# High and low weight parts in one tile, and 57 groups of dummy products behind the work

## The chip, the cores and the metric

The kernel runs on one core of one Trainium2 chip. A core has five engines that run their own instruction queues beside each other: TensorE (PE in the profile, its weight loads are PEld), VectorE (DVE), ScalarE (ACT), GpSimd (POOL) and SyncE (SP, which here only issues DMAs). They share a memory of 128 partitions (SBUF); TensorE writes its products into a second memory, PSUM, in banks of 512 float32 columns. The metric is the device time of one execution in microseconds.

## The reference

Input is a residual stream `x` of 256 rows by 4096 columns in float32. One layer runs: a normalisation, a projection to four times 4096 columns, attention with 32 heads of 128, a gate, a projection back, the residual sum, and a last normalisation.

```python
h = x + attn_branch(rms_norm(x, norm_attn), w_in_attn, w_out_attn)   # DEPTH = 1
return rms_norm(h, final_norm)

def attn_branch(xn, w_in, w_out):
    proj = xn @ w_in                       # 256 x 4096 by 4096 x 16384
    q, k, v, g = jnp.split(proj, 4, axis=-1)
    o = stick_breaking_attention(to_heads(q), to_heads(k), to_heads(v))
    return (o * jax.nn.silu(g)) @ w_out    # 256 x 4096 by 4096 x 4096
```

Nearly all of the arithmetic lies in the two large products. The convolution layer of the source isn't reached with one layer.

## The kernel before

**Products in three.** Each float32 operand is split in a high part, rounded to TensorE's 32-bit type `F32R`, and a low part, which is the rest. A product of two float32 tiles is then three products: high by high, the moving operand's low part by the stationary operand's high part, and the reverse (`mm3`). The stationary operand is a 128x128 block of the input rows ("forms": `sh`, `sl`, later `oh`, `ol`), the moving operand 512 columns of weights (`wh`, `wl`). Most steps use seven instead of eight block products, by a Strassen-like scheme, with sums of weight tiles formed on VectorE and by adding DMAs.

**Units and parts.** There are 20 units of work (`units`): 16 over the columns of the first weight matrix and 4 over the second. A unit runs through 16 steps of the inner dimension, and each step through two to four "parts" of weights. `load` brings the raw tile (`raw`, a ring of 7) by DMA; `piece` (from `split`) has ScalarE write the high part `wh[n]` and VectorE the low part `wl[n]`; `product` multiplies. Parts of two inner blocks have tag `w` in a ring of 5 (`PAIRS`), parts of one have tag `s` in a ring of 2. In the kernel before, `wh` and `wl` are two tiles with tags of their own (`wh`, `wl` of 4 KB in a partition each, for the pairs).

**Order.** The class `Plan` writes out the order of the instructions of every engine: it runs a small simulation with assumed costs and due times, and emits an instruction when its engine is free. `keep_in_program_order` then pins each instruction behind the one before it on its engine. All of these have line 121 in the profile, so groups are told apart by tile names.

**The end.** In the last unit five parts, the last five of the pairs' ring (numbers 989 to 993 of all parts), are kept until the end (`KEPT`), and their products run block by block in the order `LAST_ORDER`, so that the four result blocks finish one after the other. `last_h`, `block_done`, `part_done` and `finish` add the residual, sum squares on ScalarE, form the factor of the last normalisation (a logarithm and an exponential on ScalarE, a Newton step on VectorE), scale the rows and store them, first for rows 128 to 255 (`t` = 1), then for rows 0 to 127.

Of the kernel before, what the change touches and what calls it, by code (L numbers as in the profile page):

```python
# [10 lines left out]
F32 = mybir.dt.float32  # L11
F32R = mybir.dt.float32r
BF16 = mybir.dt.bfloat16
AF = mybir.ActivationFunctionType
ALU = mybir.AluOpType
# [4 lines left out]
P = 128  # L20
# [5 lines left out]
CW = 256  # L26
HG = CW // P
NB = D // CW
W = 2 * CW
NJ = D // W  # L30
KT = 2
# [11 lines left out]
RAW_BUFS = 7  # L43
PAIRS = 5
# [193 lines left out]
def kernel(  # L238
# [10 lines left out]
    nc = Plan(tc)  # L249
# [3 lines left out]
    wp = ctx.enter_context(tc.tile_pool(name="weights", bufs=1))  # L253
    sp = ctx.enter_context(tc.tile_pool(name="stationary", bufs=1))
    dp = ctx.enter_context(tc.tile_pool(name="spill", bufs=1, space=DRAM))
    acc = ctx.enter_context(tc.tile_pool(name="acc", bufs=1, space=PSUM))
    att = ctx.enter_context(tc.tile_pool(name="att", bufs=1, space=PSUM))
    rooms = ExitStack()
    ap = rooms.enter_context(tc.tile_pool(name="attention", bufs=1))
# [40 lines left out]
    for g, (n, k) in enumerate(order):  # L300
        p = parts[n]
        b = p["u"], p["prods"][k][0]
# [51 lines left out]
    raw, wh, wl = {}, {}, {}  # L354
# [48 lines left out]
    def sums(q):  # L403

        a, b, c, d = quad_parts[q]
        one, two = raw[q, 0], raw[q, 1]
        for k in range(2):
            tile_left[q, k] += 1

        def add(to, at_, f, g, key, op=ALU.add):  # L410
            return dve(
                lambda: nc.vector.tensor_tensor(out=to[:, :, at_, :], in0=f, in1=g, op=op), W,
                key - SUMS_AHEAD * 1e3,
            )

        yield nc.until(("lows", a), ("T3", q))
        yield add(one, 0, one[:, :, 0, :], two[:, :, 0, :], first[c], ALU.subtract)
        yield nc.until(("lows", b))
        yield add(two, 1, one[:, :, 0, :], two[:, :, 1, :], first[c])
        nc.tell(("sums", c))  # L420
        yield add(one, 1, one[:, :, 0, :], one[:, :, 1, :], first[d])
        nc.tell(("sums", d))
        for k in range(2):
            tile_done(q, k)

    def piece(n, c, there):

        p = parts[n]
        yield nc.until(*there)
        full = raw[p["tile"]][:, :, p["place"], :][:, :, c, :].rearrange("p i c n -> p c i n")  # L430
        h, l = (t[n][:, c, :].rearrange("p c (i n) -> p c i n", i=HG) for t in (wh, wl))
        size = (c.stop - c.start) * W
        key = first[n] - (AHEAD * 1e3 if p["seven"] and p["i"] < 2 else 0)
        yield act(lambda: nc.scalar.copy(h, full), size, key - 2.0 * 1e3)
        if n == 0:
            yield nc.until(("sh", c.start))
        yield dve(lambda: minus(l, full, h), size, key)
        for k in range(c.start, c.stop):
            nc.tell(("low", n, k))
        low_done(n)  # L440

    def split(size, tag, bufs):
        for n, p in enumerate(parts):
            if p["size"] != size:
                continue
            q = p["quad"]
            yield nc.take(tag)
            t = p["tile"][1]
            yield nc.until(("raw", q, t))
            wh[n] = wp.tile([P, size, W], F32R, tag=tag + "h", name=f"wh{n}", bufs=bufs)  # L450
            wl[n] = wp.tile([P, size, W], F32R, tag=tag + "l", name=f"wl{n}", bufs=bufs)
            cuts = [slice(k, k + 1) for k in range(KT)] if n == 0 else [slice(0, size)]
            lows_left[n] = len(cuts)
            if p["seven"] and p["i"] == 0:
                nc.start(sums(q))
            for c in cuts:
                nc.start(piece(n, c, [("sums", n)] if p["seven"] and p["i"] > 1 else [("raw", q, t)]))
# [112 lines left out]
    for k in range(WARM):  # L570
# [10 lines left out]
        out=bound, in_=bound, compare_op=ALU.is_gt, fill=0.0, base=0,  # L581
# [6 lines left out]
        out=tri_f, in_=tri_f, compare_op=ALU.is_ge, fill=0.0, base=0, pattern=[[-1, P]], channel_multiplier=1,  # L588
# [465 lines left out]
    def last_h():  # L1054

        u, c = LAST, NJ - 2
        bank = ev.setdefault(u, {})
        key = place_of[u + 1, 0] - (KEPT * 4 + 8) * PRODUCT
        late = place_of[u + 1, 0]
        add = lambda to, f, g, k=late, n=W: dve(  # L1060
            lambda: nc.vector.tensor_tensor(out=to, in0=f, in1=g, op=ALU.add), n, k
        )
        for d in range(2):
            yield nc.until(("used", u, LAST_STEPS[d]))
            new_h(c + d)
        for d in range(2):
            yield nc.until(("used", u, LAST_STEPS[2 + d]))
            for t in range(NT):
                yield load_out(c + d, t)
        yield nc.until(("h", c - 1))  # L1070
        for d in range(2):
            yield nc.take("gh")
            yield load_gain(c + d)
        one, two = ([hs[c + d, t] for t in range(NT)] for d in range(2))
        yield nc.until(("full", u, 1))
        yield act(lambda: nc.scalar.copy(two[0], bank[1]), W, key)
        yield act(lambda: nc.scalar.copy(one[0], bank[1]), W, key)
        yield nc.until(("full", u, 6))
        yield add(two[0], bank[6], two[0], key)
        yield nc.until(("full", u, 7))  # L1080
        yield add(two[1], bank[7], two[0], key)
        yield act(lambda: nc.scalar.copy(one[1], two[1]), W, key)
        for t, b, d in ((1, 5, 1), (1, 4, 0), (0, 2, 0), (0, 3, 1)):
            nc.start(block_done(c + d, t, b, bank, add, key + 10 * (NT - 1 - t), late))
        yield nc.until("C22")
        yield add(two[0], bank[5], two[0], late - 1)
        nc.tell("C12")
# [109 lines left out]
    def products():  # L1197
        for g, (n, k) in enumerate(order):
# [18 lines left out]
            nc.here = g * PRODUCT  # L1217

    together(split(KT, "w", PAIRS), split(1, "s", SINGLES), products(), x_stats(), x_factor(), constants())

    def in_turn(works):
# [14 lines left out]
        nc.start(again(s))  # L1236
    nc.start(last_h())
    nc.run()


# [36 lines left out]
```

## Time and profile before

| | us |
|---|---|
| time, median of 2 runs | 1740.2 (1739.15 to 1741.24) |
| span of the profiled execution, first to last instruction | 1738.8 |
| TensorE busy in it | 1722.9, 7735 products |
| VectorE busy | 1643.5 |
| ScalarE busy | 1204.9 |
| GpSimd busy | 335.5 |

The span leaves out what lies before the first and behind the last instruction; the median lies 1.4 us above it. A product's "busy" time in the profile counts from its start to its modelled end, and products overlap, so the rate of TensorE is read from the distance of their starts.

### The profile page before, as it was taken

What the parts mean: (1) busy time and instruction counts of PE and PEld (TensorE: products, weight loads), DVE (VectorE), ACT (ScalarE), POOL (GpSimd) and SP (SyncE); (2) the same over time, 40 slices, a digit from 0 to 9 for tenths busy, and PEclk for the clock granted to TensorE, in tenths of its full rate; (3) what the DMA queues carried; (4) which work ended last, traced back from release to release, by engine and by line L of the source; (5) the groups of instructions that cost most, each with busy time, mean ns of one, the idle gap of its engine ahead of it and who ended that gap; (6) DMA issues with size and microseconds to landing.
All of it is one profiled execution on the core that took longest, in us unless ns stands there. A gap on an engine that the chain in (4) does not pass through costs nothing.

```text
span 1738.8 us, 24830 instructions
## 1 busy us (share of the span) xinstructions
PE 1722.9 (99%) x7735; PEld 1412.5 (81%) x7735; DVE 1643.5 (95%) x2106; ACT 1204.9 (69%) x1640; POOL 335.5 (19%) x407
## 2 busy tenths in 40 slices
PE   9999999999999999999999999999999999999997
PEld 6888888888888888888888888888888888878885
DVE  8889999999999999999999999999999987999997
ACT  7976767676767676767676767676767675666655
POOL 0022222222222221212222222222222112221220
PEclk9999999999999999999999999999999999999999
DMA  9967788878787878787878787878787878788895
GB/s 363 297 191 227 229 231 226 230 229 236 224 234 223 240 216 238 217 251 208 255 206 255 206 256 198 257 203 259 198 256 203 269 245 265 230 268 251 233 303 191
DMA packets 249380, 413.79 MB, mean 238 GB/s; under 512 B 28128, under 2 KB 73440, under 8 KB 249248
## 3 DMA queue, kind: packets, MB, share of 16 engines
q1 hardware_dynamic: 194544, 354.24, 60.6%
q0 software_dynamic: 54416, 57.70, 20.2%
q8 instruction: 60, 0.98, 0.2%
q14 instruction: 72, 0.59, 0.1%
q10 hardware_dynamic: 288, 0.28, 0.0%
HBM read 403.98 MB, written 8.13 MB: 237 GB/s over the span
## 4 chain that ended last, share of the span: by engine, by line
PE 78%; DVE 12%; issue 6%; ACT 2%; DMA 2%; SPq 0%; DVEq 0%; ACTq 0%
PE acc L121 74%; DVE wl L121 8%; DVE raw L121 3%; PE z L121 2%; PE o L121 1%; ACT wh L121 1%; DMA raw<-in_w_in_dram 1%; PE tr L121 1%; DVE gv_sb L121 1%; DVE h L121 0%; DMA raw<-in_w_out_dram 0%; DMA grow<-in_gain_out_dram 0%; DVE qk_sb L121 0%; SPq L121 0%; ACT sq L121 0%
## 5 line engine op out<-in xcount | busy, mean ns | idle before, releaser
L121 ACT CAST wh<-raw 128x1024 fp32r<-128x1024 f32 (+1 forms) x995 | 922.0, 971 | 406.1 <-issue 180.0
L121 DVE TENSOR_TENSOR wl<-raw,wh 128x1024 fp32r<-128x1024 f32 (+1 forms) x995 | 1068.8, 1123 | 58.4 <-ACT wh L121 56.6
L121 PE MATMUL acc<-wh,sh 128*128 128x512 f32 x1898 | 755.6, 398 | 0.0
L121 PE MATMUL acc<-wl,sh 128*128 128x512 f32 x1898 | 740.0, 390 | 0.8 <-DVE wl L121 0.8
L121 PE MATMUL acc<-wh,sl 128*128 128x512 f32 x1898 | 740.5, 390 | 0.0
L121 POOL DMA_DIRECT2D raw<-in_w_in_dram x300 | 262.9, 988 | 1078.9 <-DMA raw<-in_w_in_dram 427.4
L121 PEld LDWEIGHTS acc<-wh,sl 128*128 128x128 f32 x1898 | 356.3, 188 | 75.8 <-DVE sl L121 0.4
L121 PEld LDWEIGHTS acc<-wl,sh 128*128 128x128 f32 x1898 | 357.0, 188 | 73.8 <-DVE wl L121 2.8
L121 PEld LDWEIGHTS acc<-wh,sh 128*128 128x128 f32 x1898 | 356.8, 188 | 70.7 <-ACT wh L121 0.6
L121 DVE TENSOR_TENSOR raw<-raw,raw 128x512 f32<-128x512 f32 x354 | 243.4, 687 | 6.9 <-DMA raw<-in_w_out_dram 1.2
L121 PE MATMUL acc<-wl,oh 128*128 128x512 f32 x485 | 189.7, 391 | 2.0 <-DVE wl L121 1.8
L121 PE MATMUL acc<-wh,oh 128*128 128x512 f32 x485 | 190.0, 392 | 0.0
L121 PE MATMUL acc<-wh,ol 128*128 128x512 f32 x485 | 188.9, 389 | 0.0
L121 DVE TENSOR_TENSOR raw<-raw 128x512 f32<-128x512 f32 x177 | 121.0, 684 | 0.0
L121 PEld LDWEIGHTS acc<-wl,oh 128*128 128x128 f32 x485 | 91.1, 188 | 23.8 <-DVE wl L121 5.3
L121 PEld LDWEIGHTS acc<-wh,oh 128*128 128x128 f32 x485 | 91.0, 188 | 19.2 <-DVE gv_sb L121 0.5
L121 PEld LDWEIGHTS acc<-wh,ol 128*128 128x128 f32 x485 | 91.0, 188 | 18.8
L121 POOL DMA_DIRECT2D raw<-in_w_out_dram x54 | 47.1, 968 | 185.9 <-DVE wl L121 58.9
L121 ACT ACTIVATE f<-f 128x384 f32<-128x384 f32 x96 | 50.5, 526 | 3.0
L121 ACT COPY qkT<-tr 128x512 f32<-128x512 f32 x32 | 18.6, 581 | 24.1 <-PE tr L121 24.1
L121 ACT CAST oh<-p 128x512 fp32r<-128x512 f32 (+3 forms) x46 | 20.9, 467 | 18.8 <-DVE p L121 13.2
L121 DVE SCALAR_TENSOR_TENSOR gv_sb<-acc,rin_v,gv_sb 128x512 f32<-128x512 f32 x45 | 33.4, 741 | 0.0
(91 smaller groups left out, 750.3 us busy)
## 6 DMA issues: line engine op xcount, KB each, us to landing
raw<-in_w_in_dram SPq DMA_DIRECT2D x1024, 256.0 KB, 4.5
raw<-in_w_out_dram SPq DMA_DIRECT2D x256, 256.0 KB, 4.3
raw<-in_w_in_dram POOLq DMA_DIRECT2D x300, 128.0 KB, 4.7
p<-spill POOLq DMA_DIRECT2D x28, 256.0 KB, 4.2
raw<-in_w_out_dram POOLq DMA_DIRECT2D x54, 128.0 KB, 5.1
xr<-in_x_dram SPq DMA_DIRECT2D x16, 256.0 KB, 4.8
xres<-in_x_dram SPq DMA_DIRECT2D x16, 256.0 KB, 5.6
out_dram<-h SPq DMA_DIRECT2D x16, 256.0 KB, 2.8
```

The source lines that it names most:

```text
L121: return self.tc.keep_in_program_order(getattr(self.engine, name)(*args, **kw))
```

## The change

Two things change. In `split`, high and low part of one part of weights become the two halves of one tile with one tag (8 KB in a partition for the pairs, 4 KB for the others). Behind the plan's run, a new function `probes` is called: it clears a tile, fills from it a tile `m` of 2048 columns, a tile of stationary blocks `w`, and a third tile that is written six times by ScalarE and six times by VectorE in a spread order; then it issues 57 groups of 13 products into the bank with tag `b1`. Each group reads its moving operand out of `m` by another access pattern, a list of (step, count) pairs in elements, with an offset in some. All of `m` and `w` is zero, and no later instruction reads the results.

```diff
@@ split @@
-            wh[n] = wp.tile([P, size, W], F32R, tag=tag + "h", name=f"wh{n}", bufs=bufs)
-            wl[n] = wp.tile([P, size, W], F32R, tag=tag + "l", name=f"wl{n}", bufs=bufs)
+            both = wp.tile([P, 2, size, W], F32R, tag=tag, name=f"w{n}", bufs=bufs)
+            wh[n], wl[n] = both[:, 0], both[:, 1]
@@ tile_trunk_kernel, its end @@
     nc.run()
+    probes(tc.nc, wp, acc)
+
+LANES = [
+    [(1, 512)],
+    [(16, 128), (1, 4)],
+    [(16, 128), (1, 4), 4],
...
+    [(12, 128), (1, 4)],
+    [(8, 128), (1, 4)],
+    [(4, 2), (16, 64), (1, 4)],
...
+    [(1024, 2), (16, 64), (1, 4)],
...
+    [(16, 64), (8, 2), (1, 4)],
...
+    [(16, 42), (4, 3), (1, 4)],
...
+    [(0, 128), (1, 4)],
+    [(0, 64), (4, 2), (1, 4)],
...
+    [(0, 64), (1024, 2), (1, 4)],
+    [(0, 32), (16, 4), (1, 4)],
...
+    [(16, 64), (1, 6)],
+    [(4, 4), (16, 32), (1, 4)],
+    [(16, 96), (1, 4)],
+    [(16, 126), (1, 4)],
+    [(4, 2), (16, 63), (1, 4)],
+]
+AGAIN = 13
+
+def probes(nc, wp, acc):
+    zero = wp.tile([P, HG, KT, CW], F32, tag="raw", name="zero", bufs=RAW_BUFS)
+    nc.vector.memset(zero, 0.0)
+    zero = zero.rearrange("p i k n -> p (i k n)")
+    m = wp.tile([P, 4, W], F32R, tag="w", name="probe_m", bufs=PAIRS)
+    for k in range(2):
+        nc.scalar.copy(m[:, 2 * k : 2 * k + 2].rearrange("p k n -> p (k n)"), zero)
+    m = m.rearrange("p k n -> p (k n)")
+    w, r = (wp.tile([P, 4, W], F32R, tag="w", name=f"probe_{k}", bufs=PAIRS) for k in range(2))
+    w, r, r2 = (t.rearrange("p k n -> p (k n)") for t in (w, r[:, 0:2], r[:, 2:4]))
+    nc.scalar.copy(w[:, 0:1024], zero)
+    spread = lambda t: t.rearrange("p (h q e) -> p q h e", q=4, e=4)
+    for k in range(6):
+        nc.scalar.copy(spread(r), zero.rearrange("p (q h e) -> p q h e", q=4, e=4))
+    for k in range(6):
+        nc.vector.tensor_tensor(out=spread(r2), in0=zero.rearrange(...), in1=spread(r.bitcast(F32)), op=ALU.subtract)
+    out = acc.tile([P, W], F32, tag="b1", name="probe_out")
...
+    for dims in LANES:
+        a, shape = lanes(m, dims)
+        o = out[:, 0 : math.prod(shape)]
...
+        for k in range(AGAIN):
+            nc.tensor.matmul(o, w[:, 128 * (k % 2) : 128 * (k % 2) + 128], a, start=True, stop=True, skip_group_check=True)
```

Of the 57 groups, 47 have 512 columns, 8 have 504 and 2 have 384. In the first group the columns lie one behind the other; in all others the innermost runs are of 4 columns (6 in one group), and the patterns differ in the distance and the order of these runs.

More of the change, by code (lines that the diff above doesn't have):

```diff
@@ L1238 @@
     nc.run()
+    probes(tc.nc, wp, acc)
[3 more added lines that the diff above has]
+    [(16, 128), (1, 4), 4],
+    [(16, 128), (1, 4), 8],
+    [(16, 128), (1, 4), 12],
+    [(12, 128), (1, 4)],
+    [(8, 128), (1, 4)],
+    [(4, 2), (16, 64), (1, 4)],
+    [(4, 2), (16, 64), (1, 4), 8],
+    [(8, 2), (16, 64), (1, 4)],
+    [(12, 2), (16, 64), (1, 4)],
+    [(1024, 2), (16, 64), (1, 4)],
+    [(1028, 2), (16, 64), (1, 4)],
+    [(0, 2), (16, 64), (1, 4)],
+    [(16, 64), (1024, 2), (1, 4)],
+    [(16, 64), (1028, 2), (1, 4)],
+    [(16, 64), (8, 2), (1, 4)],
+    [(16, 64), (12, 2), (1, 4)],
+    [(16, 32), (512, 4), (1, 4)],
+    [(32, 64), (16, 2), (1, 4)],
+    [(32, 64), (20, 2), (1, 4)],
+    [(16, 42), (4, 3), (1, 4)],
+    [(4, 3), (16, 42), (1, 4)],
+    [(12, 42), (4, 3), (1, 4)],
+    [(0, 128), (1, 4)],
+    [(0, 64), (4, 2), (1, 4)],
+    [(0, 64), (8, 2), (1, 4)],
+    [(0, 64), (16, 2), (1, 4)],
+    [(0, 64), (32, 2), (1, 4)],
+    [(0, 64), (64, 2), (1, 4)],
+    [(0, 64), (128, 2), (1, 4)],
+    [(0, 64), (256, 2), (1, 4)],
+    [(0, 64), (512, 2), (1, 4)],
+    [(0, 64), (1024, 2), (1, 4)],
+    [(0, 32), (16, 4), (1, 4)],
+    [(0, 16), (16, 8), (1, 4)],
+    [(0, 8), (16, 16), (1, 4)],
+    [(0, 4), (16, 32), (1, 4)],
+    [(0, 32), (4, 4), (1, 4)],
+    [(0, 32), (8, 4), (1, 4)],
+    [(0, 32), (32, 4), (1, 4)],
+    [(0, 16), (32, 8), (1, 4)],
+    [(0, 16), (4, 8), (1, 4)],
+    [(0, 8), (4, 16), (1, 4)],
+    [(0, 16), (8, 8), (1, 4)],
+    [(16, 16), (4, 8), (1, 4)],
+    [(256, 8), (16, 16), (1, 4)],
+    [(512, 4), (16, 32), (1, 4)],
+    [(1536, 2), (8, 64), (1, 4)],
+    [(16, 42), (512, 3), (1, 4)],
+    [(16, 21), (336, 6), (1, 4)],
+    [(336, 6), (16, 21), (1, 4)],
+    [(16, 64), (1, 6)],
[4 more added lines that the diff above has]
+]
@@ new lines, with lanes @@
+AGAIN = 13
[14 more added lines that the diff above has]
+    for k in range(6):
+        nc.vector.tensor_tensor(
+            out=spread(r2), in0=zero.rearrange("p (q h e) -> p q h e", q=4, e=4), in1=spread(r.bitcast(F32)), op=ALU.subtract
+        )
+    out = acc.tile([P, W], F32, tag="b1", name="probe_out")
+    def lanes(t, dims):
+        at_ = 0
+        if not isinstance(dims[-1], tuple):
+            dims, at_ = dims[:-1], dims[-1]
+        a = t[:, at_ : at_ + 1]
+        return bass.AP(tensor=a.tensor, offset=a.offset, ap=[a.ap[0], *([s, n] for s, n in dims)]), [n for _, n in dims]
+    for dims in LANES:
+        a, shape = lanes(m, dims)
+        o = out[:, 0 : math.prod(shape)]
+        if len(shape) == 2:
+            o = o.rearrange("p (a b) -> p a b", b=shape[1])
+        if len(shape) == 3:
+            o = o.rearrange("p (a b c) -> p a b c", b=shape[1], c=shape[2])
+        for k in range(AGAIN):
+            nc.tensor.matmul(
+                o, w[:, 128 * (k % 2) : 128 * (k % 2) + 128], a, start=True, stop=True, skip_group_check=True
+            )
```

## The prediction

> **What bounds the kernel now.** First the page: busy shares and the chain that ended last.
>
> ```profile
> span 1738.8 us, 24830 instructions
> PE 1722.9 (99%) x7735; PEld 1412.5 (81%) x7735; DVE 1643.5 (95%) x2106; ACT 1204.9 (69%) x1640; POOL 335.5 (19%) x407
> ...
> PE 78%; DVE 12%; issue 6%; ACT 2%; DMA 2%; SPq 0%; DVEq 0%; ACTq 0%
> ...
> L121 PE MATMUL acc<-wh,sh 128*128 128x512 f32 x1898 | 755.6, 398 | 0.0
> L121 PE MATMUL acc<-wl,sh 128*128 128x512 f32 x1898 | 740.0, 390 | 0.8 <-DVE wl L121 0.8
> L121 PE MATMUL acc<-wh,sl 128*128 128x512 f32 x1898 | 740.5, 390 | 0.0
> ```
>
> TensorE is busy 99% of the span and the chain is mostly its products, so what is appended to its queue is paid in full, and what is taken off VectorE or ScalarE is worth little. The 390 ns of a product is its length, not its price: products overlap. The price is the distance of their starts, and the timeline of TensorE over the last 24 products of the kernel shows it with nearly nothing else going on at the end:
>
> ```profile
> 1721.67 0.39 PE L121 MATMUL acc<-wh,oh 128*128 128x512 f32 x1
> ...
> 1724.16 0.39 PE L121 MATMUL acc<-wh,ol 128*128 128x512 f32 x1
> ...
> 1726.88 0.39 PE L121 MATMUL acc<-wh,ol 128*128 128x512 f32 x1
> ```
>
> From the first to the last are 23 distances in 5.21 us: **0.2265 us for 512 columns**, each product with its own weight load. That is the price of a dummy product as long as its reading pattern costs nothing.
>
> **The shared tile.** It removes and adds no instruction. Set side by side, the built programs have the same operations in the same order on all five queues up to the dummy work, SP's 1353 and GpSimd's 412 included, and the same engines are waited for, but for two VectorE instructions that no longer wait for TensorE. The reason is in the code: the high part's slot was already read last by the third product of a triple, so a slot for both comes free no later. What is left is another place of the tiles in memory. The rows above bound it: the product with the weights' low part and the second with the high part take 390 ns alike, the first 398. Those 8 ns, taken over all 2383 triples (1898 of them in this row), are 19 us, all that a better place could win by what the trace shows; I keep 19 us each way for the range and take **0**, since high and low tile read alike where only the place differs.
>
> **The setup on VectorE: 1.0 us.** The planned order puts the clearing of `zero` between the low parts of parts 988 and 989. No clear of 1024 columns is in the trace; one of 320 is, and low parts of 1024:
>
> ```profile
> L121 DVE MEMSET idle<- 128x320 uint32 x10 | 3.2, 325 | 1.7 <-PEq L1264 0.9
> ...
> L121 DVE TENSOR_TENSOR wl<-raw,wh 128x1024 fp32r<-128x1024 f32 x816 | 957.1, 1219 | 57.1 <-ACT wh L121 55.4
> ```
>
> And the timeline of VectorE, with the product that waits for its last low part:
>
> ```profile
> 1704.42 4.63 DVE L121 TENSOR_TENSOR wl<-raw,wh 128x1024 fp32r<-128x1024 f32 x4 [0.64 <-ACT wh L121]
> 1708.97 0.68 DVE L121 TENSOR_TENSOR h<-h,xres 128x512 f32<-128x512 f32 x1
> 1709.58 1.22 DVE L121 TENSOR_TENSOR wl<-raw,wh 128x1024 fp32r<-128x1024 f32 x1
> 1710.71 0.68 DVE L121 TENSOR_TENSOR h<-h,grow 128x512 f32<-128x512 f32 x1
> 1711.45 2.36 DVE L121 TENSOR_TENSOR wl<-raw,wh 128x1024 fp32r<-128x1024 f32 x2
> 1713.73 1.41 DVE L121 TENSOR_TENSOR h<-acc,h 128x512 f32<-128x512 f32 x2
> 1715.06 1.22 DVE L121 TENSOR_TENSOR wl<-raw,wh 128x1024 fp32r<-128x1024 f32 x1
> ...
> 1716.32 0.50 PE L121 MATMUL acc<-wl,oh 128*128 128x512 f32 x1
> ```
>
> 325 ns below, 1219 ns above; three times the small one is 1.0 us, which I take. It isn't hidden: the last low part ends at 1716.28 and its product starts at 1716.32, 0.1 us late already, and VectorE has hardly a gap between 1704 and 1716. So TensorE waits 1.0 us there, and the last product starts at 1727.9.
>
> **The setup on ScalarE: the dummy products start at 1729.3.** They need three copies of 1024 columns (two for `m`, one for `w`) that stand on ScalarE between the steps of the last normalisation:
>
> ```profile
> 1721.57 0.39 ACT L121 ACTIVATE sq<-h 128x256 f32<-128x256 f32 x1
> 1721.89 0.19 ACT L121 ACTIVATION_READ_ACCUMULATOR sq<-h 128x1 f32 x1
> 1722.11 0.29 ACT L121 ACTIVATE rout<-ssq_h,most 128x1 f32<-128x1 f32 x1
> 1722.44 0.20 ACT L121 ACTIVATE rout<-rout 128x1 f32<-128x1 f32 x1
> ...
> 1710.38 1.99 ACT L121 CAST wh<-raw 128x1024 fp32r<-128x1024 f32 x2
> ```
>
> The first copy stands before the logarithm of 1722.11 and takes the slot of part 989, whose last product is the one of 1724.16, over at 1724.55, with the shift 1725.6. Behind it queue the logarithm, the second copy, the exponential, the third copy: 1.0 + 0.3 + 1.0 + 0.2 + 1.0 = 3.5 us, to 1729.1, and 0.2 us to be seen and to load a weight block. ScalarE's logarithm and all that depends on it (factor, scaling, stores of rows 128 to 255) are 3 to 4 us later for it, and the twelve spread copies (six on ScalarE at 1.0 us or more, six on VectorE at 1.2 us or more) fall into the steps of rows 0 to 127. Written four times as slowly they would be some 24 and 29 us. All of that, the 16 stores too, lies beside the dummy products, which last over 150 us; without that cover it would cost about 12 us.
>
> **The dummy products: 166.0 us.** 57 groups of 13 are 741 products; 47 x 512 + 8 x 504 + 2 x 384 = 28,864 columns, times 13 is 375,232, or 732.9 products of 512 columns. At 0.2265 us: 166.0 us. The weight block alternates, so each has a load, as each product before has.
>
> What isn't in the trace is a moving operand read in runs of four. Every product of before reads its columns one behind the other. Bounds by the nearest rows, two timelines of attention steps:
>
> ```profile
> 109.95 0.22 PE L121 MATMUL z<-fh,neg_tri 128*128 128x128 f32 x1
> 110.00 0.28 PE L121 MATMUL z<-fl,neg_tri 128*128 128x128 f32 x1
> ...
> 96.86 0.60 PE L121 MATMUL tr<-ident,qk_sb 128*128 128x128 f32 x4
> 97.21 0.48 PE L121 MATMUL acc<-wh,sh 128*128 128x512 f32 x1
> 97.53 0.40 PE L121 MATMUL acc<-wl,sh 128*128 128x512 f32 x1
> ...
> L121 PEld LDWEIGHTS z<-fh,neg_tri x64: 187/188/189, 109.4 to 1417.4; 128*128 128x128 f32 x64
> ```
>
> Below: 128 columns started 0.05 us apart, 0.20 us for 512, so 147 us. Above: four transposes of 128 columns in full float32 and one product take 0.67 us, so the four 0.44 us: the slowest column rate in the trace, 322 us. I take the contiguous 0.2265. For it speaks the last row: half of those 64 weight loads read one single column with a step of 0 (the stationary operand `neg_one`), the other half a whole block, and all take 187 to 189 ns. An irregular step costs that read nothing.
>
> The Trainium skill has a rule for the read itself (SBUF — State Buffer, Specifications): lines of 16 bytes, full bandwidth with at least two hits per line, a penalty for crossing. Four float32 fill a line, so by it every group reads at the contiguous rate, and the sum stays 166 us; no row of before shows it. Its page TensorE: Matmul & The Clock Gate (Back-to-back issue gap) gives N/2.4 + 2.5 ns, 216 ns for 512 columns, and would make the sum 158 us, an estimate; the trace has 226.5, and the measurement decides.
>
> **The end.** The last product's 0.39 us reach 0.2 us past the next start that doesn't come. Behind it the core still has to close:
>
> ```profile
> 1726.37 8.71 SPq L121 DMA_DIRECT2D out_dram<-h  x11
> ...
> out_dram<-h SPq DMA_DIRECT2D x8, 256.0 KB, 2.8
> ```
>
> The last store is issued by 1735.1, at about 1734.5, lands 2.8 us later at 1737.3, and the span ends 1.5 us after that. With stores long landed I take 1.2. Span: 1729.3 + 166.0 + 0.2 + 1.2 = 1896.7, 157.9 more than 1738.8. The median of the runs lies 1.4 above that span: **1898 us**.
>
> **The rivals.**
>
> *Runs out of order cost extra, up to the full float32 rate.* For it: nothing in the trace reads so. Against: the step-0 loads. With 322 us the time is 2054; half the extra gives 1976.
>
> *The memory hands out 64 bytes at a time.* A contiguous product reads 2 KB a partition in 226.5 ns, 7.08 ns for 64 bytes. If a visit costs that however little of it is used, the 38 groups that move to another 64 bytes at each run pay 126 to 128 visits for 504 or 512 columns instead of 32, seven pay 64, two 96. 38 x 13 x 127.7 x 7.08 ns is 447 us, the others add about 88: 535 us, the time 2267. It decides from the first such group, the second of all.
>
> *The clock falls.* After the last product TensorE rests:
>
> ```profile
> 1727.00:1729.00 2.00, 0.27 (x2) 0.00 (x0) 1.17 (x5) 1.11 (x5) 0.00 (x0) 1.00 1.02 382
> 1729.00:1731.00 2.00, 0.00 (x0) 0.00 (x0) 1.49 (x7) 1.30 (x4) 0.00 (x0) 1.00 0.62 236
> 1731.00:1733.00 2.00, 0.00 (x0) 0.00 (x0) 1.71 (x3) 1.05 (x2) 0.00 (x0) 0.51 0.79 292
> ```
>
> In these stretches the third number from the right is the clock that TensorE was granted. It stays 1.00 for nearly four microseconds of rest, then is 0.5. My gap is 1 us. If the chain on ScalarE took 3 us more, a few microseconds would run at half rate, 3 us lost. Only if zeros didn't count as work would all run at half: 332 us, 2064.
>
> *The place in memory counts after all*, 19 us either way: 1879 or 1917.
>
> *Not slower: the dummy products don't run.* Nothing reads their result, and a build could drop them. Then only the copies remain: 12 us later, 1752. It decides at some 100 products left, 23 us. Against: all 741 stand in the built queue.
>
> **How the numbers follow.** Forecast, contiguous rate within some 20 us (1884 to 1918): 0.64. Extra per run: 0.18, three quarters of it below 1990. Blocks of 64 bytes: 0.13. Half clock: 0.02. Place: 0.02. Dropped: 0.01. The range starts at 1884, below which lie only a placement gain and the dropped products, and goes up to 1990 to take in the cheaper part of the second case; what lies above is just under 0.2. Two per cent are 35 us, about what a measurement of this kernel tells from no change; every case but the dropped one, and a far larger gain from the place, is slower by more: 0.98, within 0.015, faster 0.005.
>
> **What would show it.** In the profile after: 741 products of a tile `probe_out` from about 1729, the first group 0.2265 us apart and the others the same; a first group as predicted with slower ones behind it means the second or third case, by whether the extra grows with the visits. The product of 1716.32 about 1 us later shows the clearing; products before 1700 at other times than before show the place. I am wrong as well if TensorE ends long before the span does.

## The result and the profile after

The changed kernel takes **1901.1 us** (median of two runs, 1900.99 to 1901.21) against 1740.2 before: **1.092 times as long, with a 95% interval from 1.0889 to 1.0952**. The predicted 1898 us were 3 us short of it. The page of the kernel after, with the busy shares and two of TensorE's costliest groups (count, busy time, mean length of one):

```profile
span 1899.3 us, 26327 instructions
PE 1893.7 (100%) x8476; PEld 1553.4 (82%) x8476; DVE 1651.4 (87%) x2113; ACT 1212.5 (64%) x1649; POOL 334.5 (18%) x407
...
L121 PE MATMUL acc<-w,sh 128*128 128x512 f32 x3796 | 1188.2, 394 | 0.5 <-ACT w L121 0.5
...
L1340 PE MATMUL probe_out<-probe_m,probe 128*128 128x512 f32 (+2 forms) x741 | 170.4, 392 | 0.0
```

High and low parts now lie in one tile, so their products are one group of 3796. Its mean of 394 ns is the mean of the 398 and 390 of before. New is the last row: 741 products, 170.4 us of TensorE. The span grew by less, 160.5 us: in the kernel before, the last product ended at 1727.27 (1726.88 + 0.39), 11.5 us ahead of the span's end, and the closing work of these 11.5 us now lies beside the dummy products. The timeline around the seam shows the rest (start, length, and in brackets the idle time before):

```profile
1715.72 0.39 PE L121 MATMUL acc<-w,oh 128*128 128x512 f32 x1
...
1717.10 0.50 PE L121 MATMUL acc<-w,oh 128*128 128x512 f32 x1 [0.99 <-DVE w L121]
...
1722.26 0.39 PE L121 MATMUL acc<-w,ol 128*128 128x512 f32 x1
...
1722.80 1.04 ACT L1311 CAST probe_m<-zero 128x1024 fp32r<-128x1024 f32 x1
...
1724.97 1.03 ACT L1315 CAST probe<-zero 128x1024 fp32r<-128x1024 f32 x1
...
1726.29 18.44 SPq L121 DMA_DIRECT2D out_dram<-h  x16
...
1727.70 0.39 PE L121 MATMUL acc<-w,ol 128*128 128x512 f32 x1
1727.92 170.39 PE L1340 MATMUL probe_out<-probe_m,probe 128*128 128x512 f32 x741
```

Three things are to be seen. The product that takes the last low part waits 0.99 us for VectorE. ScalarE's third copy, the one that fills the weights, is over at 1726.00, so the first dummy product follows the last product of the work by 0.22 us, without a gap. And the stores are issued by 1744.7, far inside the dummy products.

How long the dummy products are is read from the windows of their tile. Each stretch here begins with the first product of a group, so its length is the sum of the distances of its starts; a count can hold one product that runs over the edge. The last stretch ends at 1897.98, just behind the start of the last product at 1897.92 (1898.31 less its 0.39), so it is 0.17 us short of a full last distance, and the table below has 11.28 for it. The columns are the stretch, its length, TensorE's busy time and count, the weight loads, the granted clock, the DMA share and GB/s:

```profile
1727.92:1730.87 2.95, 2.95 (x13) 2.44 (x13) 1.00 0.55 203
1730.87:1782.07 51.20, 51.20 (x222) 41.60 (x221) 1.00 0.17 65
1782.07:1785.53 3.46, 3.46 (x14) 2.52 (x13) 1.00 0.00 0
1785.53:1800.38 14.85, 14.85 (x66) 12.22 (x65) 1.00 0.00 1
1800.38:1828.75 28.37, 28.37 (x131) 24.63 (x130) 1.00 0.00 1
1828.75:1840.71 11.96, 11.96 (x53) 9.76 (x52) 1.00 0.00 0
1840.71:1865.76 25.05, 25.05 (x105) 19.74 (x104) 1.00 0.00 1
1865.76:1884.06 18.30, 18.30 (x79) 14.68 (x78) 1.00 0.00 1
1884.06:1886.87 2.81, 2.81 (x14) 2.49 (x13) 1.00 0.00 0
1886.87:1897.98 11.11, 11.11 (x53) 9.43 (x51) 1.00 0.00 0
```

Set against 0.2265 us for 512 columns:

| groups, counted from 0 | how they read | measured, us | at 0.2265, us | difference |
|---|---|---|---|---|
| 0 | one behind the other | 2.95 | 2.95 | 0.0 |
| 1 to 17 | runs of 4, many distances | 51.20 | 50.06 | +1.1 |
| 18 | (16, 32), (512, 4), (1, 4) | 3.46 | 2.95 | +0.5 |
| 19 to 23 | two or three runs near each other | 14.85 | 14.59 | +0.3 |
| 24 to 33 | one or two runs over and over | 28.37 | 29.45 | −1.1 |
| 34 to 37 | 4 to 32 runs, 16 columns apart, over and over | 11.96 | 11.78 | +0.2 |
| 38 to 45 | 4 to 16 runs at other distances, over and over (45 moves on instead) | 25.05 | 23.56 | +1.5 |
| 46 to 51 | blocks hundreds of columns apart | 18.30 | 17.53 | +0.8 |
| 52 | runs of 6, 384 columns | 2.81 | 2.21 | +0.6 |
| 53 to 56 | the rest | 11.28 | 10.95 | +0.3 |

No group in runs of four is far off: the slowest, group 18, takes 3.46 / 13 = 0.266 us a product, the ten groups with one or two runs 28.37 / 130 = 0.218. Group 52, in runs of six, takes 0.216 for 384 columns, 27% above the 0.170 of the sum.

### The profile page after: what moved, and what is told of

Read it like the earlier page. It is cut to its first block, busy times and chain, and to the rows that moved or that the text cites. A ratio compares the mean times of both kernels' runs of the same rounds, so it can differ in the third digit from the quotient of the medians.

```text
span 1899.3 us, 26327 instructions
## 1 busy us (share of the span) xinstructions
PE 1893.7 (100%) x8476; PEld 1553.4 (82%) x8476; DVE 1651.4 (87%) x2113; ACT 1212.5 (64%) x1649; POOL 334.5 (18%) x407
## 4 chain that ended last, share of the span: by engine, by line
PE 75%; DVE 13%; issue 6%; DMA 3%; ACT 3%; SPq 0%; DVEq 0%; ACTq 0%; POOL 0%; POOLq 0%
PE acc L121 62%; PE probe_out L1340 9%; DVE w L121 8%; DVE raw L121 3%; ACT w L121 2%; DMA raw<-in_w_out_dram 2%; PE z L121 2%; PE o L121 1%; DMA raw<-in_w_in_dram 1%; DVE gv_sb L121 1%; PE tr L121 1%; DVE h L121 0%; DMA grow<-in_gain_out_dram 0%; DVE qk_sb L121 0%; ACT f L121 0%
## 5 line engine op out<-in xcount | busy, mean ns | idle before, releaser
L121 PE MATMUL acc<-w,sh 128*128 128x512 f32 x3796 | 1188.2, 394 | 0.5 <-ACT w L121 0.5
L121 ACT CAST w<-raw 128x1024 fp32r<-128x1024 f32 (+1 forms) x995 | 921.8, 971 | 410.4 <-issue 186.7
L121 DVE TENSOR_TENSOR w<-raw,w 128x1024 fp32r<-128x1024 f32 (+1 forms) x995 | 1069.2, 1123 | 60.4 <-ACT w L121 58.6
L121 PEld LDWEIGHTS acc<-w,sh 128*128 128x128 f32 x3796 | 704.7, 188 | 143.5 <-DVE w L121 1.1
L121 PE MATMUL acc<-w,sl 128*128 128x512 f32 x1898 | 741.0, 390 | 0.0
L121 PEld LDWEIGHTS acc<-w,sl 128*128 128x128 f32 x1898 | 356.6, 188 | 75.9 <-DVE sl L121 0.4
L121 PE MATMUL acc<-w,oh 128*128 128x512 f32 x970 | 301.9, 391 | 2.6 <-DVE w L121 2.4
L121 PEld LDWEIGHTS acc<-w,oh 128*128 128x128 f32 x970 | 181.4, 188 | 43.2 <-DVE w L121 5.5
L121 PE MATMUL acc<-w,ol 128*128 128x512 f32 x485 | 188.9, 389 | 0.0
L1340 PE MATMUL probe_out<-probe_m,probe 128*128 128x512 f32 (+2 forms) x741 | 170.4, 392 | 0.0
```

The source lines that it names most:

```text
L121: return self.tc.keep_in_program_order(getattr(self.engine, name)(*args, **kw))
L1340: nc.tensor.matmul(o, w[:, 128 * (k % 2) : 128 * (k % 2) + 128], a, start=True, stop=True, skip_group_check=True)
```

## The experiments

The theory going in: the shared tile is free, the whole difference is the dummy products on TensorE's queue plus 1 us for the clear, and the 4 us beyond 166 come from the patterns. Rivals: the shared tile moves the work's own products, or the seam around the dummy products costs more than it shows.

**The shared tile alone.** The dummy work is left out; the kernel still computes the whole reference.

```
-    probes(tc.nc, wp, acc)
```

> The shared tile alone, no dummy products. My step (the shared tile costs 0, at most 19 us either way): 1740 us, a ratio of 1.000 within 0.3%, products 0.2265 us apart as before. Rival (place in memory counts): 1721 or 1759 us, and the first product of a triple at another mean length than 398 ns.

Measured: 1740.68 us (1739.9 to 1742.32), 1.0005 times before, interval 0.9996 to 1.0015. Its span and busy shares:

```profile
span 1738.8 us, 24830 instructions
...
PE 1722.7 (99%) x7735; PEld 1412.7 (81%) x7735; DVE 1643.4 (95%) x2106; ACT 1205.1 (69%) x1640; POOL 334.5 (19%) x407
```

The span is that of before to the tenth and TensorE is busy 1722.7 against 1722.9 us. No cost of the shared tile is seen, and no gain from the other place of the tiles: the interval reaches from −0.7 to +2.6 us.

**All groups read one behind the other**, with the same counts of products and columns:

```
+LANES = [[(1, n)] for n in (*[512] * 47, *[504] * 8, *[384] * 2)]
```

> As the changed kernel, but every group reads its columns one behind the other, with the same counts of columns (47 groups of 512, 8 of 504, 2 of 384). If the reading pattern is all that the sum of 166.0 us missed: dummy products take 166.0 us from first to last start, total 1897 us, 4 us less than the changed kernel. If the missing 4 us belong to something else that comes with the dummy products (instruction fetch, zeros, the writes of the spread copies beside them): 170 us again, total 1901 us.

Measured: 1898.61 us (1897.38 to 1898.98), 1.0912 times before (1.0894 to 1.093). The timeline of TensorE in this kernel:

```profile
1728.59 0.39 PE L121 MATMUL acc<-w,ol 128*128 128x512 f32 x1
1728.82 166.74 PE L1282 MATMUL probe_out<-probe_m,probe 128*128 128x512 f32 x741
```

The 741 products take 166.74 us in their row, 3.65 less than with the patterns (170.39), and 0.2 of it is the last product's tail: 166.5, the predicted 166.0 within half a microsecond. The medians are 2.5 us apart; this execution's dummy products began 0.9 us later. So the price of 0.2265 us for 512 columns was right, and what the sum lacked is the patterns.

**The clear of `zero` on GpSimd instead of VectorE:**

```
-    nc.vector.memset(zero, 0.0)
+    nc.gpsimd.memset(zero, 0.0)
```

> As the changed kernel, but the tile of zeros is cleared on GpSimd, whose queue is done by then, instead of VectorE. My step (the clear on VectorE holds up the last low part and TensorE with it): the wait of 0.99 us before the product at 1717 shrinks to the 0.1 us of before, the dummy products start about 0.9 us earlier, total 1900.2 us. Rival (the wait comes from the shared tile or from another cause): the wait stays at 1 us.

Measured: 1900.22 us in one run, span 1898.5. The timeline of TensorE, the stretch in which the kernel after waits:

```profile
1716.08 0.76 PE L121 MATMUL acc<-w,oh 128*128 128x512 f32 x2
...
1727.13 169.25 PE L1340 MATMUL probe_out<-probe_m,probe 128*128 128x512 f32 x736
```

Two products of 0.39 us started 0.227 apart would take 0.62; they take 0.76. That is no remainder of the clear: in the run with the shared tile alone, which clears nothing, the same two take as long:

```profile
1716.05 0.78 PE L121 MATMUL acc<-w,oh 128*128 128x512 f32 x2
```

So the wait went with the clear. The dummy products start 0.79 us earlier and the span is 0.8 us shorter, which fits, but would not show it alone: with the clear on VectorE, the kernel of the experiment before started them 0.9 us later than the kernel after. (This trace holds 736 of the 741 records.)

**Twice as many dummy products** (`AGAIN = 26`), to see whether the work is paid in full:

> The changed kernel with 26 instead of 13 products in each group. If all dummy work lies behind the rest of the kernel and is paid in full (my step): 170.2 us more, 2071 us, dummy products 340 us long. If part of it were hidden, or the first groups were slowed by the copies that run beside them, 2066 to 2069 us.

Measured: 2070.14 us in one run, span 2068.4. The row of the timeline:

```profile
1727.35 340.12 PE L1340 MATMUL probe_out<-probe_m,probe 128*128 128x512 f32 x1482
```

The second half adds 340.12 − 170.39 = 169.7 us to the row and 169.0 us to the time: paid in full, at full clock, with nothing hidden.

**No products, the clear and the fifteen copies stay.** The lines from `out = acc.tile(...)` to the end of `probes` are left out; the reference is still computed whole.

> The changed kernel without its dummy products; the clear and the fifteen copies stay. It measures what the dummy products cover. My step: 12 us over the kernel before, 1752 us (clear 1.0, the copies between the steps of the last normalisation the rest). If the copies don't hold up the chain of the normalisation: 1741 to 1745 us.

Measured: 1750.58 us (1749.48 to 1752.33), 1.0061 times before (1.0044 to 1.0078), so 10.3 us more. The timeline of the closing normalisation:

```profile
1723.03 1.04 ACT L1311 CAST probe_m<-zero 128x1024 fp32r<-128x1024 f32 x1
...
1725.33 0.22 DVE L121 SCALAR_TENSOR_TENSOR rout_e<-rout,mean 128x1 f32<-128x1 f32 x1 [2.01 <-ACT rout L121]
...
1726.52 18.39 SPq L121 DMA_DIRECT2D out_dram<-h  x16
```

VectorE waits 2.01 us for ScalarE's `rout`, which stands behind two of the copies. The spread copies hold up rows 0 to 127 further: of the chain that ended last, from 1715 us to the end, they are 17.2% on ScalarE and 17.4% on VectorE. In the kernel before, the last store was issued by 1726.37 + 8.71 = 1735.1; here by 1744.9. Those 9.8 us are the growth of the span (1738.8 to 1748.6). In the kernel after the stores end at the same place (1744.7) and cost nothing, because 150 us of dummy products still follow.

**What a pattern costs: weights by moving operand.** The table above does not say whether the moving operand's own reads or their meeting with the weight loads make the differences. Here 48 other groups of 13 take the place of the 57, without the spread copies: six ways to read the weights (`turn` the two blocks in turn, `same` one block, `one` a single column 128 times, `off` one block 4 columns further, `each` every 4th, then every 16th column) by seven ways to read the moving operand, and six groups of other widths.

```
+WEIGHTS = {"turn": None, "same": [(1, 128)], "one": [(0, 128)], "off4": [(1, 128), 4], "each4": [(4, 128)], "each16": [(16, 128)]}
+MOVES = {"run": [(1, 512)], "still": [(0, 128), (1, 4)], "two": [(0, 64), (4, 2), (1, 4)], "lane0": [(16, 128), (1, 4)],
+         "lane1": [(16, 128), (1, 4), 4], "far": [(16, 32), (512, 4), (1, 4)], "rows4": [(0, 32), (32, 4), (1, 4)]}
+MORE = {"n128": [(1, 128)], "n256": [(1, 256)], "n384": [(1, 384)], "half": [(4, 128), (1, 2)], "lhalf": [(16, 128), (1, 2)], "still2": [(0, 256), (1, 2)]}
```

> As the changed kernel with other dummy groups and no spread copies: six ways to read the weight block (alternating blocks, the same block, one column with step 0, the block four columns further, every 4th column, every 16th column) times seven moving patterns (in a row; one run of four again and again; two runs of four in turn; runs of four with step 16 at offset 0 and 4; runs of four out of four far places; four rows of 32 in turn), then alternating blocks with 128, 256, 384 columns in a row and with runs of two. Theory A (the time over 213 ns comes from the weight load reading memory beside the moving operand): with one weight column in a row goes from 227 to about 215 to 218 ns, and with every 4th or 16th column, 128 lines instead of 32, all patterns rise by 10 ns or more. Theory B (it belongs to the moving read alone): 227 in a row, 218 for two runs in turn and 260 or so for the far places, whatever the weights. Runs of two: 256 columns in 128 lines take about 215 ns if a line costs the same however much of it is used, 113 ns if columns count.

Measured: 1893.69 us in one run. Each row of the timeline below is one group of 13, named by weights and moving operand; the profile leaves out numbers in names, so the `each` rows before 1849 are every 4th column and the later one every 16th. Every group has an output tile of its own, and from the second group on its first distance holds about 0.1 us of waiting (but not `turn_run`'s, the first), so a length less that and less the last product's 0.39 us, divided by 12, is about the distance (with spread weights the first wait is about 0.2 us):

```profile
1728.86 3.11 PE L1299 MATMUL turn_run<-pm,pw 128*128 128x512 f32 x13
1732.03 3.11 PE L1299 MATMUL turn_still<-pm,pw 128*128 128x512 f32 x13
...
1745.06 3.80 PE L1299 MATMUL turn_far<-pm,pw 128*128 128x512 f32 x13
1748.92 3.58 PE L1299 MATMUL turn_rows<-pm,pw 128*128 128x512 f32 x13
1752.55 3.25 PE L1299 MATMUL same_run<-pm,pw 128*128 128x512 f32 x13
...
1776.38 3.24 PE L1299 MATMUL one_run<-pm,pw 128*128 128x512 f32 x13
...
1824.56 3.46 PE L1299 MATMUL each_run<-pm,pw 128*128 128x512 f32 x13
1828.07 3.41 PE L1299 MATMUL each_still<-pm,pw 128*128 128x512 f32 x13
...
1853.38 3.21 PE L1299 MATMUL each_still<-pm,pw 128*128 128x512 f32 x13
...
1881.45 3.24 PE L1299 MATMUL turn_half<-pm,pw 128*128 128x256 f32 x13
```

With the weights untouched the moving operand alone makes the difference between 0.218 (`turn_still`), 0.227 (`turn_run`) and about 0.27 (`turn_far`). A weight load of one single column does not make reading in a row any faster: `one_run` is at (3.24 − 0.39 − 0.1) / 12 = 0.229, as is `same_run` with a whole block. But the weights are not out of it: weights from every 4th column lengthen both the run and the still read by 0.2 to 0.3 us a group, of which 0.12 is a longer first wait and the rest lies between the products. The still read goes from 0.219 to 0.233 us a product by the starts in the trace, the read in a row from 0.229 to 0.237. Weights from every 16th column, which by the first theory should have slowed all patterns, leave the still read at 0.219. Neither "the moving reads alone" nor "the meeting with the weights alone" fits. The last row is the outcome that the expectation named for a price by the line: 256 columns that use half of each 16 bytes take as long as 512 columns that use all of them.

**The place of the weights, and reads that straddle.** One weight block for all 13 products of a group, at seventeen places (`from_a` to `from_q`: columns 0, 2, 4 ... 96) and with thirteen steps (`step_b` to `step_n`: 2 to 16); the moving operand from other places; and 126 runs of four columns that lie within 16 bytes or across two of them.

```
+FROM = dict(a=0, b=2, c=4, d=6, e=8, f=10, g=12, h=14, i=16, j=20, k=24, l=28, m=32, n=48, o=64, p=80, q=96)
+STEP = dict(b=2, c=3, d=4, e=5, f=6, g=7, h=8, i=9, j=10, k=12, l=14, m=15, n=16)
...
+    "across": [(16, 126), (1, 4), 2],
+    "within": [(16, 126), (1, 4)],
+    "pairs": [(4, 2), (16, 64), (1, 4)],
```

> As the changed kernel with other dummy groups and no spread copies, the same weight block in all 13 products of a group. A product of 512 columns in a row is read beside weight blocks of 128 columns in a row that begin 0 to 96 columns from the tile's start (from_a to from_q), beside weights at steps 2 to 16 (step_b to step_n); then one weight block beside moving operands that begin elsewhere or are read in runs. The run before gave 0.4167 ns a column and 13.3 ns on top for 256, 384 and 512 columns. Theory P (the 13.3 ns are collisions of the weight load's reads with the moving reads, so they hang on where the two lie against each other): distances between 218 and 240 ns that change with the first column of the weights or of the moving operand, repeating with some period; a place below 220 would be worth up to 7 ns on 7149 products, 50 us of the kernel. Theory F (a fixed cost of each product): 227 ns at every place. Runs of four that lie across two lines of 16 bytes (across): 252 visits instead of 126; 440 ns if each visit of a line has the price that contiguous reading gives it, 1.77 ns; 224 to 240 as within one line if columns count.

Measured: 1913.72 us in one run. The rows of the timeline:

```profile
1728.12 3.11 PE L1298 MATMUL from_a<-pm,pw 128*128 128x512 f32 x13
...
1734.62 3.29 PE L1298 MATMUL from_c<-pm,pw 128*128 128x512 f32 x13
...
1774.79 3.25 PE L1298 MATMUL from_o<-pm,pw 128*128 128x512 f32 x13
...
1816.56 3.87 PE L1298 MATMUL step_k<-pm,pw 128*128 128x512 f32 x13
...
1861.23 5.80 PE L1298 MATMUL across<-pm,pw 128*128 128x504 f32 x13
1867.09 3.29 PE L1298 MATMUL within<-pm,pw 128*128 128x504 f32 x13
...
1875.43 3.18 PE L1298 MATMUL pairs<-pm,pw 128*128 128x512 f32 x13
```

Place counts, but little, and only for the worse: with 0.1 us off for the first wait, `from_c` is at 0.233 and `from_o` at 0.230, and no place is below the 0.227 of `from_a`, which is what the work's products already have. Part of even that is not place: `same_run` of the experiment before reads the same columns as `from_a`, stands behind another group instead of first, and is at 0.229. The weights' step counts more: every 12th column (`step_k`) lengthens the group to 3.87 us, 0.268 us a product by the starts in the trace. By far the most is made by straddling: the same 504 columns in runs of four take 5.80 us instead of 3.29 when each run lies across a limit of 16 bytes. And one pattern is a little faster than reading in a row: `pairs`, at (3.18 − 0.49) / 12 = 0.224.

**The work itself read in that pattern.** If `pairs` saves some 3 ns a product, the kernel without dummy work could be faster than before. Here the shared tile is laid out in rows of 16 columns, 8 of the high and 8 of the low part, so that a product reads two runs of four in each row. No dummy work; the reference is computed whole.

```
-            wh[n], wl[n] = both[:, 0], both[:, 1]
+            wh[n], wl[n] = (
+                both.rearrange("p a k n -> p (a k n)").rearrange("p (b a i e) -> p a i b e", a=2, i=HG, e=4)[:, a] for a in range(2)
+            )
...
-            (wh[n][:, c, :], wl[n][:, c, :]),
+            tuple(t[n][:, :, 64 * c : 64 * c + 64, :] for t in (wh, wl)),
```

> No dummy products; the shared tile is laid out in rows of 16 columns, runs of four of the high part in the first half of a row, of the low part in the second. The work's own products then read their moving operand by the dummy pattern (4, 2), (16, 64), (1, 4), at offset 0 for the high and 8 for the low part, and ScalarE and VectorE write in such runs. If the distances of the dummy groups hold for the work's products (222.5 to 223.8 ns at offset 0 and 226.5 to 227.7 at offset 8 against 226.7 in a row): 5 to 9 ns a triple on 2383 triples, 11 to 20 us less, 1720 to 1729 us. If the weight blocks of the work, which begin at other places, change the distance as they did for reading in a row (230 to 234 ns): 1740 to 1790 us. Writes cost what they did before in either case (1.05 and 1.22 us for 1024 columns).

Measured: 1737.58 us (1736.2 to 1739.85) against 1739.72 of before on the same chip: 0.9987 times, interval 0.9978 to 0.9996. The groups by shape, then the end of TensorE's timeline:

```profile
L121 PE MATMUL acc<-w,sh 128*128 128x512 f32 x3796 | 1178.4, 390 | 0.9 <-ACT w L121 0.8
...
L121 DVE TENSOR_TENSOR w<-raw,w 128x1024 fp32r<-128x1024 f32 x816 | 956.8, 1218 | 57.8 <-ACT w L121 56.8
...
L121 ACT CAST w<-raw 128x1024 fp32r<-128x1024 f32 x816 | 824.3, 1048 | 336.8 <-issue 141.4 <-PE acc L121 125.6 <-DVE raw L121 55.7
```

```profile
1724.71 0.38 PE L121 MATMUL acc<-w,ol 128*128 128x512 f32 x1
```

The last product starts at 1724.71 instead of 1726.88, so the 2.1 us are TensorE's. The spread writes cost VectorE and ScalarE nothing: 1218 and 1048 ns, as before. It is a gain by its interval, well below 2%, and far under the 11 us and more that were expected.

The starts in this trace and in that of the shared tile alone say where the rest is. Over the 1898 triples with the stationary forms `sh` and `sl` (distances under 0.3 us), the first product of a triple, which reads the high part from column 0 of each row, takes 223.8 ns on average instead of 228.5. It does as well as its dummy group did (222.5 to 223.8). The second, which reads the low part from column 8, takes 228.3 instead of 227.2, and the third 227.3 instead of 227.4. That is 3.7 ns a triple where 5 to 9 were expected; over all distances, counted up to 0.3 us each, it is 6.9 us. What the distances exceed 0.3 us by, TensorE's waits, grew from 12.7 to 17.3 us and took 4.7 of it back; in the eight other traces these waits of the work are 12.4 to 14.1. Why they grew, no run isolates; that VectorE, busy 95% of the time, leaves little room is a guess.

## Why the prediction was right

The time was 3 us above the forecast and well inside the range. By its own steps:

- **The bound.** Appended work was paid in full: a second set of the same products adds 169.0 us to the time.
- **The shared tile, 0 (19 us kept either way).** Right, and the 19 us were far too careful: without dummy work it measures 1.0005 times before (0.9996 to 1.0015). The 398 ns of the first product stayed, as the mean of 394 shows; it is a length in the trace that the other place of the tiles did not remove.
- **The clear, 1.0 us.** Right in place and size: the product behind the last low part waits 0.99 us, and with the clear on GpSimd the wait is gone. The clear itself is short of a microsecond (this row is from the groups of the kernel after):

```profile
L1307 DVE MEMSET zero<- 128x1024 f32 x1 | 0.9, 912 | 0.3 <-DVE w L121 0.3
```

- **The setup on ScalarE, start at 1729.3.** This is the step that failed, by 1.4 us: the start was 1727.92. The prediction had the first copy wait for the slot of part 989, until 1725.6. It started at 1722.80, right behind the last sum of squares. In the program's order part 990 is read last 24 products before the end, by the product that starts at 1722.26 and is over at 1722.65; part 989 is still read after that. So the tile took the slot that came free first. That fits the times; which slot it is, no row shows by name. Without that wait the three copies lie wholly beside TensorE's last products, and ScalarE's setup costs the path nothing. The first store is issued 2.4 us later than before (1726.29 against 1723.86), where 3 to 4 were expected.
- **The dummy products, 166.0 us.** The term that was mis-sized: from 1727.92 to 1898.31 they take 170.4 us, 170.2 without the tail of 0.2, so +4.2. Read in a row they take 166.5, hence the product price was right, and taking 0 for the patterns was not: between −1.1 and +1.5 us for a set of groups, +4 in all. Of the two bounds, the lower (0.05 us for 128 columns) rested on the distance of one pair of products and is no rate: the `turn_n` group of 128 columns, weights by moving operand, has 0.11 us between its starts. The step-0 weight loads that spoke for 0 were weak evidence, since the moving operand is another read. The rule of the Trainium skill (SBUF — State Buffer, Specifications), by which runs of four should read at full rate, holds to within −4% and +18% here (0.218 and 0.266 against 0.2265 us), so the sum it supports was near enough. Where it says that two hits per line suffice, the trace disagrees: 256 columns that use half of each line took the time of 512.
- **The end, 0.2 + 1.2.** It took 0.2 + 1.0 (1898.31 to 1899.3).
- **The sum.** −1.4 + 4.2 − 0.2 is +2.6, the 1899.3 of the span against 1896.7. The median lies 1.8 above the span where 1.4 was taken. The two larger misses partly cancelled, so the forecast looks better than its steps.
- **The rivals.** Extra per run, up to the float32 rate: there is an extra, but 4 us of it and not 78 or more; the slowest group takes 0.266 us a product where that rate would give 0.44. Blocks of 64 bytes: out by the same group, as such a group of 128 visits would take 0.9 us a product; the limit that does cost is that of 16 bytes. The clock: 1.00 in every stretch. Place: nothing beyond the 2.6 us of the interval. Products dropped: all 741 are there. And the cover, put at 12 us if it were gone, is worth 10.3.

## What to carry to other kernels

Price appended work on the bounding engine by the distance of starts, not by the length of an instruction, and check first whether its setup ends before that engine's last useful instruction: then only its own queue counts. Do not take the oldest tile for the free slot: the times here fit the slot that the order of the work releases first, so read the wait from that order. For the moving operand of a product, keep each run of four float32 columns inside its 16 bytes and use all of them; the order of the runs moved the time by −4% to +18% here, straddling costs nearly a factor of two.

## What the runs showed of the hardware

- **Lines of 16 bytes are paid for, however much of them is used.** Runs of four within a line: 3.29 us for 13 products; across two lines: 5.80. The products of the second group (count, shortest, median and longest length in ns, first and last start):

```profile
L1298 PE MATMUL across<-pm,pw x13: 600/603/679, 1861.2 to 1866.4; 128*128 128x504 f32 x13
```

  The twelve distances make 5.2 us, the first of them 0.50 by the trace, so 252 lines take 0.427 us a product; 126 lines, within, take 0.232. That is 1.7 to 1.85 ns for each line that the read moves to. Full lines in a row fit that too (128 lines in 0.227), and so do half-used lines (3.24 us for 256 columns in 128 lines) and the runs of six, which touch 128 lines with 384 columns (0.216). Reading 256 columns one behind the other is much quicker, as the view of that tile in the experiment on weights by moving operand shows (in the same columns):

```profile
L1299 PE MATMUL turn_n<-pm,pw x11: 280/282/389, 1877.0 to 1878.3; 128*128 128x256 f32 x11
```

  Ten distances in 1.3 us: about 0.13 us a product with the first wait, 0.12 without.
- **Staying in a line is hardly cheaper than moving on.** The ten groups of one or two runs over and over take 0.218 us, a little less than reading in a row. With a single run the read never leaves its line, so lines are not the whole price: there is one for columns too. That the longer of the two decides would fit these rows; no run tests it by itself.
- **Four rows taken in turn cost more.** With a run of four out of each of four rows in turn, rows 512 columns apart take about 0.27 us a product (`turn_far`, and 0.266 in group 18 of the kernel after), but rows only 32 columns apart take about 0.255 as well (`turn_rows`). Why stays open: no run here varied the distance finely enough.
- **The weights' read counts.** With the moving operand in a row, the weight block at column 0 leaves 0.227 to 0.229 us between products, at column 4 0.233, and with every 12th column 0.268. A spread load is slower in itself, whatever the moving operand: loads of a block in a row last 188 to 191 ns, those of every 12th column 363, and beside the still read those of every 4th and every 16th column (in this order) 328 and 291:

```profile
L1299 PEld LDWEIGHTS each_still<-pm,pw x13: 309/328/330, 1828.1 to 1830.9; 128*128 128x128 f32 x13
...
L1299 PEld LDWEIGHTS each_still<-pm,pw x13: 291/291/310, 1853.4 to 1856.0; 128*128 128x128 f32 x13
```

  The second of these does not slow the still read at all (0.219), so a longer load need not cost the products anything. The Trainium skill (TensorE: Matmul & The Clock Gate, Step-by-step: what each phase is for) says that loading the next weights takes no read bandwidth from the running product. For a block read in a row that is near the truth here. For spread blocks the products get slower beside many moving reads, as beside the read in a row; whether the load takes reads from them or holds them up by its length was not told apart.
- **Spread writes cost nothing here.** With the parts laid out in runs (the last experiment), VectorE's low parts take 1218 ns, against 1219 before, and ScalarE's high parts 1048.
